# A feed-forward that starts on a quarter of its modulation, and attention with v as the stationary operand

## The chip, the core and the metric

The kernel runs on one core of a Trainium2 chip. The metric is the device time in microseconds (us) from the first to the last instruction of one launch. Each engine (TensorE for matmuls, VectorE, ScalarE, GpSimd, and SyncE, which issues DMAs) works through its own queue in the order in which the program gives it instructions; semaphores make one wait for another.

## The reference

One step of a small diffusion backbone of two layers: 256 latent and 128 context tokens of width 1024 (three tiles of 128 tokens, NT = 3). Per layer: a SwiGLU feed-forward, a mixer (layer 0 attention, layer 1 a gated recurrence) and a second feed-forward, each between two RMS norms and with a modulation made from a conditioning vector. What the change touches is the first feed-forward and the attention:

```python
mod = (silu(c) @ w_ada[i] + b_ada[i])                  # shift, scale, gate for three sub-layers
h = rmsnorm(x, g_pre) * (1 + scale) + shift            # D_MODEL = 1024
a, b = split(h @ w_in);  out = (silu(a) * b) @ w_out   # D_FF = 2816
# attention: 16 query heads of 64, 4 key/value heads, one softmax with a sink per head
s = concat([q @ k_window.T, q @ k_ctx.T]) * 64 ** -0.5
m = maximum(max(s), sink);  e = exp(s - m)
o = (e @ v) / (sum(e) + exp(sink - m))
```

Latent queries see 256 latent keys (masked to a window) and 128 cached context keys, so 384 keys; context queries see 128.

## The kernel before

**Weights.** All big weights are streamed through one list, `chunks`, of 512 KB pieces, each a 128x1024 tile. SyncE loads a chunk into a raw buffer (L172); `w_split` makes two parts of it, `wh` on ScalarE (L198, a rounded copy) and `wl` on VectorE (L199, the rest; on GpSimd where `ws["eng"]` says so), and a product in nearly full precision is three matmuls of the rounded parts (`mm3`, L451 to L453). `take` gives the next chunk and splits it if that has not been done; `prefetch` splits some chunks ahead. Chunks in `plain` are used as they are. The first NE chunks go through ten buffers (`early`: one raw, three slots, three `araw`, `gbr`, two raws), the later ones through three raws; a buffer is loaded anew when its last reader is done.

**The start.** `start` loads x and the conditioning, normalises x and turns it (`normalise`, `lay`), and computes shift and scale of the first feed-forward in two halves of 512 features: `gather` (sixteen plain chunks of `w_ada`, two matmuls each into 32-partition rows of a PSUM bank), an evacuation on ScalarE (L1430), `spread` (four tiny matmuls that turn the rows into columns), then `modulate_first` (scale and shift on VectorE L1458, rounded copy on ScalarE L1463, rest on VectorE L1467). Two feed-forward chunks that need only the first half run before the second half's modulation (`between`), a third is used as filler (`fill`).

**The feed-forward.** 44 chunks of `w_ffn_in`, each 24 matmuls of 128x384, in 11 groups of four; after each group a gate (silu and product). Then 22 chunks of `w_ffn_out`. Between the chunks `pace` puts pieces of the other modulations: a unit (`ada_unit`) multiplies a 128x1024 tile of `w_ada` by a column and adds it up on VectorE (L247); sixteen units are one kind, and a kind ends with a rows matmul (L272), an evacuation and small DMAs. `set_pace` gives the number of kinds that should be ready: 5 in the first feed-forward, 5.5 and 6 in attention.

**Attention.** After the projections (`qkv_part`, `q_evac`, `kd_turn`) the queries are turned (`q_turn`). The loop runs over 36 items: 16 single heads of tile 0, four items of four heads of the context tile, 16 heads of tile 1. For an item: `score` (two matmuls and a mask, TensorE), `top` and `shift` (maximum, VectorE), `expo` (ScalarE, with the sum), `flip` (transposes of e, TensorE, and the evacuation to `pT` on ScalarE, L954), `weigh` (pT is the stationary operand, v moves, 64 columns each). Scores run two items ahead, exponentials one. After eight heads `o_prep`, `o_norm` (division, L977), `o_turn` (transposes), `o_hi`, `o_lo` bring the output into `hT`.

## Time and profile before

| | |
|---|---|
| median of three runs | 1585.67 us (1583.9 to 1587.08) |
| the profiled execution | 1587.23 us, its span 1585.5 us |
| mean granted TensorE clock | 0.995 |
| TensorE busy | 1549.3 us, 98% of the span |
| VectorE busy | 1046.4 us, 66% |
| ScalarE busy | 651.6 us, 41% |

The span is the time from the first to the last instruction of the profiled execution. An engine's busy time is the time in which at least one of its instructions was running.

### The profile page before, as it was taken

How to read it: one execution, taken by the hardware profiler on the slowest of the kernel's cores; microseconds unless marked ns; L12 is line 12 of the kernel's file. 1: busy time of each engine (PE TensorE's matmuls, PEld its weight loads, DVE VectorE, ACT ScalarE, POOL GpSimd, SP SyncE). 2: the span in 40 equal slices, each digit the busy share in tenths (PEclk: the TensorE clock that was granted, in tenths of full speed). 3: DMA queues.
4: the chain of work that ended last, by engine and by line, in shares of the span. 5: the costliest groups of instructions: out<-in, count | busy, mean ns of one | idle time of the engine just before them, and what ended most of it. 6: DMA issues, size and time to landing. Idle time of an engine off the chain costs nothing.

```text
span 1585.5 us, 22547 instructions
## 1 busy us (share of the span) xinstructions
PE 1549.3 (98%) x8798; PEld 1414.8 (89%) x8798; DVE 1046.4 (66%) x1388; ACT 651.6 (41%) x1118; POOL 161.7 (10%) x308
## 2 busy tenths in 40 slices
PE   6999999998999999999999999999999999999997
PEld 4899998887879999988999998899999889999985
DVE  3787788577756777785688889666666764333452
ACT  3423233365745322334523233356655443323441
POOL 1111111000011111120111111110000110000000
PEclk9999999999999999999999999999999999999999
DMA  8777667342224766665377776634333335433321
GB/s 307 245 242 219 221 214 239 120 146 81 67 94 138 218 216 206 207 215 180 114 235 228 227 236 229 227 106 134 101 113 100 121 113 163 130 126 127 131 96 40
DMA packets 164091, 264.50 MB, mean 167 GB/s; under 512 B 10432, under 2 KB 122144, under 8 KB 163984
## 3 DMA queue, kind: packets, MB, share of 16 engines
q1 hardware_dynamic: 140592, 187.27, 36.4%
q0 software_dynamic: 22864, 75.36, 14.8%
q8 instruction: 69, 1.13, 0.3%
q10 hardware_dynamic: 528, 0.43, 0.1%
q14 instruction: 38, 0.31, 0.1%
HBM read 260.01 MB, written 3.01 MB: 166 GB/s over the span
## 4 chain that ended last, share of the span: by engine, by line
PE 92%; DVE 4%; ACT 2%; issue 1%; DMA 0%; POOL 0%; DVEq 0%; POOLq 0%; ACTq 0%
PE pb L451 14%; PE pb L452 14%; PE pb L453 14%; PE pb L461 14%; PE pb L463 13%; PE pb L466 13%; PE pb L963 1%; PE pb L272 1%; PE pb L953 1%; PE pb L923 1%; PE pb L1132 1%; DVE slot L247 1%; PE pb L434 1%; DVE wl L199 1%; PE pb L1428 1%
## 5 line engine op out<-in xcount | busy, mean ns | idle before, releaser
L198 ACT ACTIVATE wh<-raw 128x1024 fp32r<-128x1024 f32 x247 | 259.8, 1058 | 413.2 <-PE pb L466 254.8
L461 PE MATMUL pb<-hT,wh 128*128 128x384 f32 (+1 forms) x1248 | 410.2, 332 | 0.0
L199 DVE TENSOR_TENSOR wl<-raw,wh 128x1024 fp32r<-128x1024 f32 x245 | 298.5, 1223 | 167.7 <-ACT wh L198 167.2
L463 PE MATMUL pb<-hT,wl 128*128 128x384 f32 (+1 forms) x1248 | 406.5, 329 | 0.0
L247 DVE SCALAR_TENSOR_TENSOR slot<-araw,sc,slot 128x1024 f32<-128x1024 f32 x224 | 281.5, 1279 | 0.0
L466 PE MATMUL pb<-hT,wh 128*128 128x384 f32 (+1 forms) x1248 | 259.8, 329 | 0.0
L461 PEld LDWEIGHTS pb<-hT,wh 128*128 128x128 f32 x1248 | 234.8, 188 | 6.2 <-issue 5.9
L463 PEld LDWEIGHTS pb<-hT,wl 128*128 128x128 f32 x1248 | 234.9, 188 | 0.2
L466 PEld LDWEIGHTS pb<-hT,wh 128*128 128x128 f32 x1248 | 215.8, 188 | 0.0
L451 PE MATMUL pb<-wh,gh 128*128 128x512 f32 x384 | 150.6, 392 | 0.2 <-DVE dump L282 0.2
L452 PE MATMUL pb<-wl,gh 128*128 128x512 f32 x384 | 149.6, 389 | 0.0
L453 PE MATMUL pb<-wh,gl 128*128 128x512 f32 x384 | 149.5, 389 | 0.0
L233 POOL DMA_DIRECT2D araw<-in_w_ada_dram x128 | 68.7, 537 | 578.0 <-DVE slot L247 480.6
L451 PE MATMUL pb<-hT,wh 128*128 128x384 f32 x352 | 119.7, 340 | 4.9 <-ACT hT L1463 4.9
L452 PE MATMUL pb<-hT,wh 128*128 128x384 f32 x352 | 119.0, 338 | 0.2 <-DVE hT L1467 0.2
L453 PE MATMUL pb<-hT,wl 128*128 128x384 f32 x352 | 118.6, 337 | 0.0
L199 DVE TENSOR_TENSOR wl<-araw,wh 128x1024 fp32r<-128x1024 f32 x52 | 63.6, 1224 | 68.3 <-ACT wh L198 68.3
L451 PE MATMUL pb<-wh,hT 128*128 128x512 f32 (+1 forms) x258 | 94.3, 365 | 1.1 <-ACT sgn L1242 0.9
L453 PE MATMUL pb<-wh,hT 128*128 128x512 f32 (+1 forms) x258 | 90.7, 352 | 0.0
L452 PE MATMUL pb<-wl,hT 128*128 128x512 f32 (+1 forms) x258 | 90.6, 351 | 0.0
L451 PEld LDWEIGHTS pb<-wh,gh 128*128 128x128 f32 x384 | 72.1, 188 | 19.4 <-issue 3.4
L453 PEld LDWEIGHTS pb<-wh,gl 128*128 128x128 f32 x384 | 72.1, 188 | 15.2
(242 smaller groups left out, 2177.8 us busy)
## 6 DMA issues: line engine op xcount, KB each, us to landing
raw<-in_w_ffn_in_dram SPq DMA_DIRECT2D x155, 512.0 KB, 4.4
araw<-in_w_ada_dram POOLq DMA_DIRECT2D x128, 512.0 KB, 4.4
raw<-in_w_ffn_out_dram SPq DMA_DIRECT2D x76, 512.0 KB, 4.2
raw<-in_w_rec_in_dram SPq DMA_DIRECT2D x21, 512.0 KB, 3.6
araw<-in_w_ffn_in_dram SPq DMA_DIRECT2D x21, 512.0 KB, 3.5
araw<-in_w_rec_in_dram SPq DMA_DIRECT2D x19, 512.0 KB, 3.7
slot<-dsc POOLq DMA_DIRECT2D x24, 256.0 KB, 5.2
raw<-in_w_qkv_dram SPq DMA_DIRECT2D x12, 512.0 KB, 4.1
```

The source lines that it names most:

```text
L198: S.activation(out=h, in_=r, func=AF.Copy)
L199: ws["eng"].tensor_tensor(out=lo, in0=r, in1=h.bitcast(F32), op=ALU.subtract)
L233: G.dma_start(out=araw[j % NA], in_=w_ada[kd[0], (j % 8) * P:(j % 8 + 1) * P, acol(kd):acol(kd) + 1024])
L247: V.scalar_tensor_tensor(out=acc[v], in0=src, scalar=s_, in1=acc[v], op0=ALU.mult, op1=ALU.add)
L272: T.matmul(out=bank[32 * r:32 * r + 32, :], lhsT=ones, rhs=acc[v][:, 512 * h:512 * h + 512], start=True, stop=True, skip_group_check=True,)
L434: T.transpose(bks[half][:, k * P:(k + 1) * P], src[:, kk * P:(kk + 1) * P], ident)
L451: T.matmul(out=out, lhsT=a[0], rhs=b[0], start=start, stop=False, skip_group_check=True)
L452: T.matmul(out=out, lhsT=a[0], rhs=b[1], start=False, stop=False, skip_group_check=True)
L453: T.matmul(out=out, lhsT=a[1], rhs=b[0], start=False, stop=stop, skip_group_check=True)
L461: T.matmul(out=out, lhsT=a[0], rhs=b[0], start=start, stop=False, skip_group_check=True)
L463: T.matmul(out=out, lhsT=x, rhs=y, start=False, stop=False, skip_group_check=True)
L466: T.matmul(out=out, lhsT=x, rhs=y, start=False, stop=stop, skip_group_check=True)
```

## The change

In the start, shift and scale are made in four quarters of 256 features instead of two halves: a plain chunk now holds four k-blocks of 256 columns, a `gather` is four matmuls of 256 columns, and one bank (PB[7]) holds both kinds. `between` is written out by hand: it takes the eight chunks of the first two groups (f00 to f03 and f10 to f13, the first digit the group) and runs `unit`s, six matmuls over the two k-blocks of one quarter. x is loaded on SyncE's queue ahead of the chunks, no longer on GpSimd's. NE is 22. The first feed-forward makes six kinds of modulation, attention none.

In attention `weigh` runs once per eight heads, with v (128x64) as stationary operand and 512 columns of `pT` moving; the result is already turned, so 1/den is spread over 64 columns, transposed (`o_row`) and multiplied in (`o_mul`) before `o_hi` and `o_lo`. Scores run three items ahead, exponentials two; two of five evacuations of `flip` go to VectorE; the first three scores are put between the last three `qkv_part`s of the context tile, and six of the query transposes into the loop (`q_turn4`). The rows of `w_attn_out` come in another order, in two DMAs per chunk.

```diff
-NE = 18
-PLAIN = tuple(range(8)) + tuple(range(10, 18))
+NE = 22
+PLAIN = tuple(6 * q + i for q in range(4) for i in range(4))
...
+    for q in range(4):
         for kind in (1, 0):
+            col = kind * 1024 + 256 * q
+            early_chunks += [av[0][:, 4 * h:4 * h + 4, col:col + 256] for h in range(2)]
+        early_chunks += chunks[4 * (q % 2) + 2 * (q // 2):][:2]
...
+            if isinstance(c_, tuple):
+                for q in range(2):
+                    SP.dma_start(out=raw_of(j)[64 * q:64 * q + 64, :], in_=c_[q])
...
+            def unit(gi, s, m, w, kq):
...
+                for k in (2 * kq, 2 * kq + 1):
+                    group.append((bank(gi, m, s)[:, 0:TOK], (wv[0][:, k % 4, ms], wv[1][:, k % 4, ms]), (hT[:, :, 0, k, :], hT[:, :, 1, k, :]),
+                                  k == 0, k == KD - 1))
+                mm3s(group, "a")
...
-        set_pace(5.5, 9)
+        set_pace(6, 5)
...
-            def weigh(i):
...
-                            out=bank(6 + h // 8)[:, (h % 8) * 64:(h % 8) * 64 + 64], lhsT=src[:, o:o + P],
-                            rhs=v_sb[:, k0 + j, (h // 4) * 64:(h // 4) * 64 + 64], start=j == 0, stop=j == n - 1,
+            def weigh(t, gp, c):
+                n, k0 = (3, 0) if t < 2 else (1, 3)
+                for j in range(n):
+                    for q in range(2):
                         T.matmul(
+                            out=bank(6 + c % 2)[64 * q:64 * q + 64, :], lhsT=v_sb[:, k0 + j, (2 * gp + q) * 64:(2 * gp + q) * 64 + 64],
+                            rhs=pT[c % 2][:, 4 * q:4 * q + 4, j, :], start=j == 0, stop=j == n - 1, skip_group_check=True,
...
+                if i % 5 in (1, 3):
+                    V.tensor_copy(out=dst, in_=src)
+                else:
+                    S.activation(out=dst, in_=src, func=AF.Copy)
...
+            def o_mul(t, gp, c):
+                u = half_of(slots[oslot], c % 2)
+                S.activation(out=u, in_=bank(5), func=AF.Copy)
+                V.tensor_tensor(out=u, in0=u, in1=bank(6 + c % 2), op=ALU.mult)
...
+                    for lag, step, fn in ((0, 1, o_prep), (1, 0, weigh), (1, 1, o_den), (3, 0, o_row), (3, 1, o_mul), (4, 0, o_hi), (4, 1, o_lo)):
...
+            for i in range(3):
                 score(i)
                 top(i)
                 shift(i)
+                if i > 0:
+                    expo(i - 1)
+                qkv_part(2, 1 + i, ww[i], sets[2][2])
...
             for i in range(n + 1):
+                if i + 2 < n:
+                    expo(i + 2)
                 if i < n:
                     flip(i)
+                if i + 3 < n:
+                    score(i + 3)
                 fire(i, 0)
+                if i + 3 < n:
+                    top(i + 3)
+                    shift(i + 3)
                 fire(i, 1)
...
+        def between(unit, gate):
+            ws["eng"] = G
+            (f00,) = take()
+            ws["eng"] = V
+            modulate_first(0)
+            (f01,) = take()
+            laid(1)
+            for s, w in ((0, f00), (1, f01)):
+                for m in range(2):
+                    unit(0, s, m, w, 0)
+            for i in range(4):
+                gather(1, i, 0)
+            (f10,) = take()
+            unit(1, 0, 0, f10, 0)
+            spread(1)
+            unit(1, 0, 1, f10, 0)
             modulate_first(1)
+            (f11,) = take()
+            unit(1, 1, 0, f11, 0)
+            for m in range(2):
+                unit(0, 0, m, f00, 1)
+            for i in range(4):
+                gather(2, i, 0)
+            for m in range(2):
+                unit(0, 1, m, f01, 1)
+            spread(2)
+            for s, m, w in ((0, 0, f10), (0, 1, f10), (1, 0, f11)):
+                unit(1, s, m, w, 1)
+            (f02,) = take()
+            modulate_first(2)
+            (f03,) = take()
+            for s, w in ((0, f02), (1, f03)):
+                for m in range(2):
+                    unit(0, s, m, w, 2)
+            for i in range(4):
+                gather(3, i, 0)
+            (f12,) = take()
+            for m in range(2):
+                unit(1, 0, m, f12, 2)
+            spread(3)
+            modulate_first(3)
+            for kq in range(2):
+                unit(1, 1, 1, f11, kq)
+            (f13,) = take()
+            w_split(24, 12)
+            for s, w in ((0, f02), (1, f03)):
+                for m in range(2):
+                    unit(0, s, m, w, 3)
+            gate(0, TOK)
+            w_split(26, 18)
+            for m in range(2):
+                unit(1, 1, m, f13, 2)
+            for s, w in ((0, f12), (1, f13)):
+                for m in range(2):
+                    unit(1, s, m, w, 3)
+            gate(1, TOK)
...
-        done = ffn(0, 0, 5, None, [0, 1, 2, 3], between)
+        done = ffn(0, 0, 6, None, [0, 1, 2, 3], between)
```

## Rows read from the trace of the kernel before

**Rows 1.** The page, part 4: the chain of work that ended last, shares of the span by engine.
```profile
PE 92%; DVE 4%; ACT 2%; issue 1%; DMA 0%; POOL 0%; DVEq 0%; POOLq 0%; ACTq 0%
```

**Rows 2.** Stretches of the start: from and to (us), length, busy time (and instructions) of each engine, granted TensorE clock, DMA share, GB/s.
```profile
0.00:10.00 10.00, 2.13 (x5) 0.27 (x5) 1.84 (x4) 3.82 (x10) 3.73 (x14) 1.00 0.76 267
...
20.00:30.00 10.00, 6.14 (x34) 4.06 (x35) 5.86 (x16) 3.85 (x11) 2.34 (x1) 0.81 1.06 382
```

**Rows 3.** Timeline of the start: start (us), duration, engine, line, operation, tiles, count, in brackets the idle time of the engine just before and what ended it.
```profile
7.64 1.88 PE L1428 MATMUL pb<-raw,sc 128*2 128x512 f32 x4 [0.27 <-DVE sc L1419]
...
19.06 0.60 ACT L1430 ACTIVATE slot<-pb 128x512 f32<-128x512 f32 x1 [6.42 <-PE pb L1428]
...
22.62 0.60 ACT L1430 ACTIVATE slot<-pb 128x512 f32<-128x512 f32 x1 [2.48 <-PE pb L1428]
...
24.24 2.34 POOL L199 TENSOR_TENSOR wl<-raw,wh 128x1024 fp32r<-128x1024 f32 x1 [10.57 <-ACT wh L198]
...
26.83 1.13 ACT L1463 ACTIVATE hT<-slot 128x256 fp32r<-128x256 f32 x4 [2.66 <-DVE slot L1458]
...
27.49 0.69 PE L451 MATMUL pb<-hT,wh 128*128 128x384 f32 x1 [3.17 <-ACT hT L1463]
...
33.26 0.34 PE L453 MATMUL pb<-hT,wl 128*128 128x384 f32 x1
...
38.46 0.34 PE L453 MATMUL pb<-hT,wl 128*128 128x384 f32 x1
...
38.73 0.60 PE L1428 MATMUL pb<-raw,sc 128*2 128x512 f32 x2
...
41.42 1.05 PE L1437 MATMUL pb<-cf,slot 128*128 128x2 f32 x8
...
50.43 0.45 PE L451 MATMUL pb<-hT,wh 128*128 128x384 f32 x1 [1.71 <-ACT hT L1463]
...
53.78 0.34 PE L451 MATMUL pb<-hT,wh 128*128 128x384 f32 x1
```

**Rows 4.** Timeline, one split of a chunk and one pair of modulated blocks (columns as in rows 3).
```profile
30.10 1.04 ACT L198 ACTIVATE wh<-raw 128x1024 fp32r<-128x1024 f32 x1
...
31.17 1.23 DVE L199 TENSOR_TENSOR wl<-raw,wh 128x1024 fp32r<-128x1024 f32 x1 [0.30 <-ACT wh L198]
...
50.95 0.66 DVE L1458 TENSOR_SCALAR slot<-slot,slot 128x256 f32<-128x256 f32 x2
...
51.39 0.62 ACT L1463 ACTIVATE hT<-slot 128x256 fp32r<-128x256 f32 x2 [0.50 <-DVE slot L1458]
```

**Rows 5.** The page, part 6: DMA issues by tile, count, KB each, median us from issue to landing.
```profile
raw<-in_w_ffn_in_dram SPq DMA_DIRECT2D x155, 512.0 KB, 4.4
...
raw<-in_w_rec_in_dram SPq DMA_DIRECT2D x21, 512.0 KB, 3.6
```

**Rows 6.** One head of the steady loop in the chain of waits (start, us on the chain, what), and the groups of the loop's stretch, 383.5 to 447.5 us, on ScalarE and VectorE (busy us, mean ns of one, idle time before them and what ended it).
```profile
391.55 0.33 PE pb L953 x3
391.88 0.34 PE pb L923 x2
392.30 0.67 PE pb L963 x6
...
L943 ACT ACTIVATE p<-pb,nm 128x384 f32<-128x384 f32 x32 | 18.6, 580 | 11.3 <-DVE nm L935 10.6 <-DVE den L975 0.6
L930 DVE TENSOR_REDUCE mx<-pb 128x1 f32<-128x384 f32 x32 | 17.8, 555 | 12.1 <-PE pb L926 11.8
L954 ACT ACTIVATE pT<-pb 128x384 f32<-128x384 f32 x32 | 15.6, 487 | 0.3 <-PE pb L953 0.3
```

**Rows 7.** Timeline of ScalarE in the loop: an evacuation, an exponential, an evacuation, each right behind the other.
```profile
423.27 0.48 ACT L954 ACTIVATE pT<-pb 128x384 f32<-128x384 f32 x1
...
423.64 0.58 ACT L943 ACTIVATE p<-pb,nm 128x384 f32<-128x384 f32 x1
...
424.19 0.50 ACT L954 ACTIVATE pT<-pb 128x384 f32<-128x384 f32 x1
```

**Rows 8.** Timeline of TensorE around the loop: the last query transposes ahead of the context tile's query parts, the flips of items 8, 16, 20 and 28, and the first product of the output projection.
```profile
372.05 1.94 PE L885 MATMUL pb<-cf,qs 128*128 128x128 f32 x16
...
397.25 0.50 PE L953 MATMUL pb<-cf,p 128*128 128x128 f32 x3
...
410.12 1.34 PE L953 MATMUL pb<-cf,p 128*128 128x128 f32 x4
...
420.14 0.55 PE L953 MATMUL pb<-cf,p 128*128 128x128 f32 x3
...
434.54 0.49 PE L953 MATMUL pb<-cf,p 128*128 128x128 f32 x3
...
447.54 0.48 PE L451 MATMUL pb<-wh,hT 128*128 128x512 f32 x1
```

**Rows 9.** Timeline of TensorE at a rows matmul: four matmuls of 512 columns (two records each) on four groups of 32 columns, and the operation behind them.
```profile
449.11 1.06 PE L272 MATMUL pb<-slot,ones 128*32 128x512 f32 x8
450.11 0.50 PE L451 MATMUL pb<-wh,hT 128*128 128x512 f32 x1
```

**Rows 10.** Stretches of the first feed-forward at the turn to its output half (columns as in rows 2; the third busy time is VectorE's).
```profile
210.00:230.00 20.00, 19.84 (x113) 18.00 (x112) 19.03 (x25) 8.86 (x15) 3.74 (x7) 1.00 0.62 204
230.00:250.00 20.00, 20.00 (x90) 16.54 (x89) 17.57 (x19) 7.39 (x10) 2.74 (x5) 1.00 0.71 239
```

More of the change, by code (lines that the diff above doesn't have):

```diff
@@ L620, in products @@
                     groups.append(group)
-                if side:
-                    mm3s([g_ for pair in zip(*groups) for g_ in pair], None)
-                    return
                 for group in groups:
@@ L663, in ffn @@
             n = 0
[L664 removed]
             while n < len(order):
[L666 removed]
+                gi, kp = order[n]
                 if n == len(order) - 2:
@@ L705, in ffn @@
                 prefetch()
-                products(gi, kp, w, 0, NT, side=n == 3 and between is not None)
+                products(gi, kp, w, 0, NT)
                 if n == 4 and between is None:
@@ L1398, in start @@
         G.memset(mhalf, -0.5)
-        for kind in range(2):
-            V.memset(PB[6 + kind], 0.0)
+        V.memset(PB[7], 0.0)
         S.activation(out=stat[:, 0, :], in_=ones[:, 0:8], func=AF.Silu)
```

283 lines of the change are left out of this document (116 added, 167 removed).

## Prediction

> **What bounds the kernel now.** I read the page's chain of waits first: TensorE holds 92% of what ended last [rows 1]. A change pays only where TensorE stands still, runs at its lower clock, or does fewer matmuls. Next I read the timeline of the two stretches that the diff touches.
>
> In the start the reader is to see that the first product of the feed-forward (a 128x384 matmul, L451) runs at 27.49 us, the fourth chunk's first at 50.43, and that from 53.78 the products follow one another without a gap [rows 3]. Two chunks of 24 and two halves of 12 (72 products) precede 50.43, and 15 more 53.78. At 0.173 us each (the 18th starts at 33.26, the 48th at 38.46), eight chunks (192 products, what the new opening holds) are through at 53.78 + 105 x 0.173 = 72.0 us. That is the mark for the opening.
>
> In attention the marks are the sixteen transposes that end at 373.7 and the first product of the output projection at 447.54, 73.8 us later [rows 8]. In the steady part the chain is TensorE's alone: per head transposes 0.33, scores 0.34 (0.42 with the mask), weighing 0.67, together 1.43 [rows 6]. The weighing is the dearest.
>
> **The change: the opening.** Bytes and sums stay: 16 chunks of modulation weights, 16 x 2 x 512 columns of gathers, four spreads. What changes is their order.
>
> *First product.* The three x blocks (1.57 MB) now go ahead of chunk 0 on SP's queue. In the first 10 us 2.67 MB arrived [rows 2], so 2.1 MB are there at about 8.5, usable near 9.5 (estimate), against a first gather at 7.6 before. Four gathers and three layings then take TensorE about 8.2 us, less than the 11.4 of before (7.6 to 19.06) because nothing waits for x and four column groups run at a time. The evacuation of the first quarter falls at 18.0 to 18.3 instead of 22.62 for both kinds. From that evacuation the way is as before: wh on ScalarE 1.05, wl on GpSimd 2.34 during which VectorE's L1458 stands (first pair free only at 26.83), then the product: 27.49 - 22.62 = 4.87 [rows 3]. So 23.0 us, 4.5 earlier; I allow 22.3 to 24.
>
> *From there I walk along TensorE's order.* Prices: product 0.173; gather 0.45 a chunk (six chunks from 38.73 to 41.42); spread 1.0; evacuation 0.6; wh 1.05 and wl 1.23 with some 0.1 of hand-over; per pair of modulated blocks 0.66 on VectorE, 0.62 on ScalarE [rows 3, 4]. No chunk is split ahead any more: each take() stands right before its use, behind the evacuation or the modulation in ScalarE's order.
> - 24 products of quarter 0. The first 17 were slow after 27.49 (until 33.26, 5.8 us; the granted clock was 0.81 on the mean of that stretch, a mix of 1.2 and 2.4 GHz [rows 2, 3]); the idle ahead is like that of before, so again: 23.0 + 5.8 + 7 x 0.173 = 30.0.
> - Four gathers 1.8: 31.8. Then f10's wh stands behind the evacuation: **wait 1.8**; four products, **wait 0.6** for wl, two products, spread, six products: 37.2.
> - f11's wh stands behind all of modulate_first(1): from the spread's end 0.1 + 0.6 (three small operations) + 0.66 + 0.62 + 0.62 + 1.05 + 0.1 = 3.75, of which six products cover 1.04: **wait 2.7**, then **0.6** for wl: 41.6.
> - 12 products, gathers, 12, spread, 18 products: 51.6. Quarter 2's blocks come 0.1 + 0.6 + 1.23 (f02's wl ahead of them on VectorE) + 0.66 + 0.62 after the spread, nearly hidden under the 18: **wait 1.1** in all; 24 products: 56.9.
> - Gathers 1.8: 58.7. f12 is chunk 22, and its buffer (raws[1]) is that of chunk 19, which the second of these gathers reads. So its DMA starts at 57.8, lands 3.6 later (the quickest median; 4.4 is the commonest [rows 5]), and needs 1.05 of ScalarE: **wait 3.9**, then **0.6**; 12 products, spread, 12 products of f11: 68.4.
> - **Wait 1.3** for quarter 3's blocks, 24 and 36 products: 80.1.
>
> So 80.1 against 72.0: **8.1 us later**. The sum of its parts: first product -4.5; waits behind it 12.6 against 2.7 before (1.9 ahead of 50.43 and 0.8 behind it); three spreads and twelve gathers instead of two and eight, +2.8; that is 8.2. If the 3.9 us wait is followed by the slow clock as the 3.2 us one ahead of 27.49 was (the 1.9 us one ahead of 50.43 was not), 2.4 more. I take 8.5, with 4 (landing at 3, two waits half hidden) and 12 (slow clock, the ada DMAs of GpSimd in the way of f12) as ends.
>
> **The change: pacing.** Attention loses 16 units of modulation (1.28 us each on VectorE); the first feed-forward has 96 instead of 80 on 36 instead of 41 chunk steps. VectorE is busy 19.0 of 20 us at the turn to the output half and 17.6 after it [rows 10], and gets 10% more work: about full. Cover: weights are split up to four chunks (16 us) ahead, so I price it at nothing; uncovered it costs up to 3 us. The rows matmul of the sixth kind (1.0 us, [rows 9]) moves with it, no gain. The output weights now come in two DMAs a chunk: eight issues more on SP, whose queue is nearly idle there; nothing to 0.5 us.
>
> **The change: attention.** *Weighing.* Before, 6 records of 64 columns a head, 0.67. After, for eight heads 6 matmuls of 512 columns with v stationary, in pairs on two halves of the array's columns. No row shows halves; the nearest are four matmuls of 512 columns on four column groups, 1.0 us from the first to the next operation [rows 9]. Side by side a pair costs 0.9: 2.7 for eight heads instead of 5.4, and 12.6 instead of 25 for the whole loop. One after the other 1.8 each: no gain. I take 0.9. *Added:* per eight heads two small VectorE copies (0.3 each), one more ScalarE copy (0.5); 2 of 5 evacuations go from ScalarE to VectorE. *Moved:* three scores and six of the query transposes go into and under the loop, with three query parts (1.38 each) between the scores.
>
> TensorE's work from 373.7 on thus falls to 51 us: transposes 12.5, scores 16.7, query parts 4.1, query transposes 2.6, weighing 12.6, transposes of 1/den 2.6. But it has to be fed in order: exp(i+2), copy(i) on ScalarE; top, shift, some copies on VectorE. Per group of eight heads ScalarE needs 8 x 0.56 + 5 x 0.38 + 1.2 = 7.6 us, VectorE 8 x 0.60 + 3 x 0.47 + 2.4 = 8.6 (0.56 and 0.38 from start to start [rows 7]; VectorE's 0.60 is its reduction and what follows it [rows 6]), TensorE 9.2; every one of them is near the bound. And the weighing is now one block of 2.7 us that stands between flip(i) and flip(i+1): ScalarE has two exponentials and a copy ready (1.5 us), then waits 1.5 for the flip and 0.8 for the next shift; the normalisation goes ScalarE, VectorE, ScalarE, VectorE, each in its queue's order, some 2 us more of waits. I wrote the loop down queue by queue with these durations, each operation starting when its queue and its inputs are free. The loop of before comes out so at 64.6 us, where the trace has 64.0. The new one, from 373.7:
> - until flip 8: 15.9 (before: 397.25 - 373.7 = 23.5): **-7.6**, the fill of the pipe and the query transposes;
> - flip 8 to 16: 14.0 (12.9); 16 to 20: 8.9 (10.0); 20 to 28: 15.5 (14.4); 28 to the end: 15.2 (13.0) [rows 8]: **+3.3**, as the block's waits eat what the cheaper weighing gives.
>
> So 69.5 against 73.8: **-4.3 us**. Ends: -18 (no engine waits, below) and +6 (pairs in series: the same walk with 1.8 gives 79.8).
>
> This is where a rule speaks against the change. The Trainium skill, TensorEngine Tiling (Array Packing), Performance Considerations (PSUM Bottleneck), says that tiling quickens TensorE but not the evacuation of PSUM, which may become the bottleneck. By that rule alone the loop could not end before VectorE's 45 us (36 maxima, 14 evacuations, two splits, six times 2.4) and its waits are through, which is what my walk has; no run here shows it yet.
>
> **Sum.** The profiled execution took 1587.23 us, 1.56 above the median shown. 1587.2 + 8.5 - 4.3 = 1591.4; against the median 1589.9, so **1590 us**. Measurement tells about 0.2%, 3.2 us.
>
> **Rivals.**
> - *The loop runs at TensorE's pace* (the other side). If three scores and two exponentials ahead are enough to bridge the 2.7 us block, the loop needs 51 + some 4 of filling and ending: 18 to 19 us less; with the opening at +8.5, 1576. For: each engine's sum is below 9.3 a group. Against: ScalarE and VectorE are in order and trade four times per group. It decides from a loop of 62 us on (373.7 to about 436). Chance 0.17.
> - *The opening is even* (its waits are covered, say because f12 lands in time): -4.3 alone, 1581.5. Against: the order of take() on ScalarE. Chance 0.12.
> - *The two cancel*: opening +5, attention -5, 1586. Chance 0.18.
> - *Pairs in series*: +8.5 + 6, 1600. For: no row with halves; against: the four groups ran together. Chance 0.10.
> - *My forecast*, 1587 to 1596: 0.43.
>
> The range 1576 to 1600 leaves out half of the first and of the fourth. My own case alone has its 1587 to 1596. Faster by over 0.2%: the first, the second less a third, 0.25. Within: the third and a slice of mine, 0.25. Slower: the rest, 0.50.
>
> **What would show it.** Opening right: first product near 23, then waits of 1.8, 2.7 and 4 us from about 32, 37 and 59 on, the last ending on a DMA of w_ffn_in; 192 products through near 80 to 82. Attention right: the weighing's pairs 0.9 apart, an eight-head group of 13 to 15 us, TensorE's transposes waiting for ScalarE's and VectorE's copies. Wrong: f12's weights there before the fourth gather, or TensorE without gaps in the loop; then the time falls below 1582.

## The result and the profile after

The changed kernel takes 1605.2 us (median of four runs, 1604.8 to 1606.3), the kernel before 1586.4 (four runs): ratio 1.0125, 95% interval 1.0113 to 1.0138. It is 19 us slower, and the forecast of 1590 us (1576 to 1600) missed it on the fast side. The profiled execution took 1605.46 us, its span 1603.7, the mean granted clock 0.985 (before 0.995). The chain of waits, by engine (compare [rows 1]: TensorE held 92%, DMAs 0%):

```profile
PE 90%; DVE 3%; ACT 2%; issue 2%; DMA 2%; POOL 0%; SPq 0%; DVEq 0%; POOLq 0%; ACTq 0%
```

**Where the time went.** I cut both traces at six marks of TensorE (start times) and compare the stages.

| stage | ends at (before, after) | length before | after | difference |
|---|---|---|---|---|
| to the first product | 27.49, 22.31 | 27.49 | 22.31 | -5.2 |
| to the record with the 192nd product | 71.80, 85.44 | 44.31 | 63.13 | +18.8 |
| rest of the input half | 227.31, 241.25 | 155.51 | 155.81 | +0.3 |
| output half of the first feed-forward | 321.17, 346.11 | 93.86 | 104.86 | +11.0 |
| attention, to the output projection | 447.54, 468.60 | 126.37 | 122.49 | -3.9 |
| output projection, to the third eight turns of the next norm | 494.33, 513.90 | 46.79 | 45.30 | -1.5 |

A row of the trace can hold two products: in the new order the 191st and the 192nd stand in one row, whose start counts, 0.17 us early. Behind the last mark the distance stays (1234.52 and 1254.07 at a wait in the recurrence) but for 1.4 us at the very end. These 1.4 are not the change's: from that wait to the end the profiles of all kernels here show either 349.3 to 349.7 or 350.7 to 351.0 us, with the old parts and with the new. So the opening costs 13.6 us and the output half 11.0, and attention with its projection gives 5.4 back.

*The opening.* Timeline of the changed kernel's start (columns as in [rows 3]; L464 to L469 are the products there, L201 the rounded copy of a split, L1440 the spread, L175 and L236 the loads of SP and GpSimd), then stretches of it (columns as in [rows 2]).

```profile
22.31 0.69 PE L464 MATMUL pb<-hT,wh 128*128 128x384 f32 x1 [3.59 <-ACT hT L1469]
...
32.61 0.44 PE L464 MATMUL pb<-hT,wh 128*128 128x384 f32 x1 [1.66 <-ACT wh L201]
33.87 1.01 PE L469 MATMUL pb<-hT,wl 128*128 128x384 f32 x2 [0.30 <-DVE wl L202]
34.67 1.70 PE L1440 MATMUL pb<-cf,slot 128*128 128x2 f32 x8
...
39.52 0.69 PE L464 MATMUL pb<-hT,wh 128*128 128x384 f32 x1 [1.02 <-ACT wh L201]
...
56.33 1.83 POOL L236 DMA_DIRECT2D araw<-in_w_ada_dram  x3
58.80 1.49 SPq L175 DMA_DIRECT2D raw<-in_w_ffn_in_dram  x3
64.53 1.06 ACT L201 ACTIVATE wh<-raw 128x1024 fp32r<-128x1024 f32 x1 [4.20 <-DMA raw<-in_w_ffn_in_dram]
65.64 0.69 PE L464 MATMUL pb<-hT,wh 128*128 128x384 f32 x1 [6.03 <-ACT wh L201]
71.86 0.69 PE L464 MATMUL pb<-hT,wh 128*128 128x384 f32 x1 [0.52 <-DVE slot L1450]
...
85.44 0.51 PE L469 MATMUL pb<-hT,wl 128*128 128x384 f32 x2
```

```profile
30.00:40.00 10.00, 7.02 (x41) 5.46 (x32) 4.45 (x13) 3.68 (x7) 0.00 (x0) 0.69 0.97 312
40.00:50.00 10.00, 10.00 (x71) 8.54 (x71) 0.72 (x1) 1.55 (x2) 0.00 (x0) 0.80 0.18 56
...
60.00:70.00 10.00, 4.36 (x15) 4.24 (x15) 1.22 (x1) 1.39 (x2) 0.00 (x0) 0.73 0.86 302
70.00:80.00 10.00, 9.48 (x46) 9.39 (x46) 5.90 (x15) 5.69 (x10) 0.00 (x0) 0.76 0.26 76
```

The reader sees each wait of the walk: 1.66 for f10, 1.02 for f11, 6.03 for f12, whose load starts at 58.80, behind three loads of GpSimd at 56.33, and is there at 64.5. And the reader sees what the walk had nearly left out: behind the waits for f10 and for f12 the clock falls (at the one for f11 it is down already). Between 30 and 80 us the granted clock is 0.69 to 0.80 in four of five stretches (a mix of 1.2 and 2.4 GHz), and a spread takes 1.70 us instead of 1.05 [rows 3].

*The output half.* The two waits of the changed kernel (timeline; L454 is the product, L275 the rows matmul of a kind).

```profile
244.78 0.50 PE L454 MATMUL pb<-wh,gh 128*128 128x512 f32 x1 [1.98 <-DVE dump L285]
310.80 3.08 PE L275 MATMUL pb<-slot,ones 128*32 128x512 f32 x8 [3.96 <-DVE slot L250]
```

One stretch of it, in the changed kernel and then in the kernel before (columns as in [rows 2]).

```profile
250.00:300.00 50.00, 50.00 (x224) 40.17 (x223) 44.16 (x48) 19.54 (x26) 9.59 (x18) 1.00 0.75 258
```

```profile
250.00:300.00 50.00, 50.00 (x224) 40.17 (x223) 30.93 (x35) 18.34 (x26) 6.72 (x13) 1.00 0.59 193
```

VectorE's costliest group from the first output product to the first product of attention, after and before (columns as in [rows 6]).

```profile
L250 DVE SCALAR_TENSOR_TENSOR slot<-araw,sc,slot 128x1024 f32<-128x1024 f32 x27 | 33.6, 1278 | 0.0
```

```profile
L247 DVE SCALAR_TENSOR_TENSOR slot<-araw,sc,slot 128x1024 f32<-128x1024 f32 x14 | 17.5, 1278 | 0.0
```

The output half has 27 of these units instead of 14; VectorE is busy 44.2 of 50 us instead of 30.9. TensorE never waits for split weights there. It waits for a modulation that nobody needs yet: at the rows matmul, which stands in its queue, until VectorE has done the last unit (4.0 us), and for a bank that VectorE has still to read (2.0). The 1.06 us matmul of [rows 9] then takes 3.08: the granted clock is 0.53 there, and its second pair starts 1.2 us after the first, since it needs one unit more. Of the 11.0 us, 5.8 are standing still (5.9 against 0.2), 1.1 is the rows matmul that moved here, and the rest, some 4, is mostly the lower clock around the two waits (0.81 on the mean from 241 to 250 us, 0.96 from 300 to 346; an estimate).

*Attention.* The marks of [rows 8] in the changed kernel, in order of time: sixteen transposes, flips 8 and 16, the second weighing of eight latent heads (L956, six matmuls in twelve records), flips 20 and 28, the third weighing, the last one, the first product of the output projection.

```profile
396.99 1.91 PE L877 MATMUL pb<-cf,qs 128*128 128x128 f32 x16
...
414.86 0.50 PE L944 MATMUL pb<-cf,p 128*128 128x128 f32 x3
...
428.71 0.66 PE L944 MATMUL pb<-cf,p 128*128 128x128 f32 x4 [1.02 <-ACT qs L950]
...
430.14 3.64 PE L956 MATMUL pb<-qs,v_sb 128*64 128x512 f32 x12
...
437.95 0.50 PE L944 MATMUL pb<-cf,p 128*128 128x128 f32 x3
...
452.26 0.50 PE L944 MATMUL pb<-cf,p 128*128 128x128 f32 x3
...
453.11 2.98 PE L956 MATMUL pb<-qs,v_sb 128*64 128x512 f32 x12
...
463.84 4.82 PE L956 MATMUL pb<-qs,v_sb 128*64 128x512 f32 x12
468.60 0.50 PE L454 MATMUL pb<-wh,hT 128*128 128x512 f32 x1
```

From the transposes' end (396.99 + 1.65, as 372.05 + 1.65 before): 16.2 to flip 8, then 13.9, 9.2, 14.3 and 16.3, together 70.0; the walk had 15.9, 14.0, 8.9, 15.5, 15.2, together 69.5. The four weighings take 2.9, 3.6, 2.9 and 4.8 us to the next operation, where 2.7 was the price; the second runs at full clock (1.00), the last at a granted clock of 0.64, behind three waits of the loop's end. TensorE waits 8.7 us in this stretch, 6.5 of them for the evacuations of flip on ScalarE (L950) and VectorE (L948); from 373.7 to 447.54 in the kernel before it waits 5.9 us, none of it for the evacuation of flip (L954). Its waits from 398.6 to 468.6 us (us in total, times, longest):

```profile
PE pb L944 <- ACT qs L950: 4.7, 6, 1.2
PE pb L944 <- DVE qs L948: 1.8, 3, 0.8
```

### The profile page after: what moved, and what is told of

Read it like the earlier page. It is cut to its first block, busy times and chain, and to the rows that moved or that the text cites. A ratio compares the mean times of both kernels' runs of the same rounds, so it can differ in the third digit from the quotient of the medians.

```text
span 1603.7 us, 22376 instructions
## 1 busy us (share of the span) xinstructions
PE 1549.7 (97%) x8694; PEld 1405.4 (88%) x8694; DVE 1053.6 (66%) x1420; ACT 648.9 (40%) x1110; POOL 158.3 (10%) x304
## 4 chain that ended last, share of the span: by engine, by line
PE 90%; DVE 3%; ACT 2%; issue 2%; DMA 2%; POOL 0%; SPq 0%; DVEq 0%; POOLq 0%; ACTq 0%
PE pb L464 14%; PE pb L466 14%; PE pb L469 14%; PE pb L454 13%; PE pb L456 13%; PE pb L455 13%; PE pb L275 1%; PE pb L956 1%; DVE slot L250 1%; DMA raw<-in_w_ffn_out_dram 1%; PE pb L1134 1%; PE pb L406 0%; PE pb L1426 0%; DVE wl L202 0%; ACT wh L201 0%
## 5 line engine op out<-in xcount | busy, mean ns | idle before, releaser
L464 PE MATMUL pb<-hT,wh 128*128 128x384 f32 (+1 forms) x1312 | 436.4, 336 | 12.8 <-ACT wh L201 8.7
L201 ACT ACTIVATE wh<-raw 128x1024 fp32r<-128x1024 f32 x242 | 254.6, 1058 | 411.6 <-PE pb L469 255.6
L202 DVE TENSOR_TENSOR wl<-raw,wh 128x1024 fp32r<-128x1024 f32 x242 | 294.5, 1223 | 157.9 <-ACT wh L201 155.2
L464 PEld LDWEIGHTS pb<-hT,wh 128*128 128x128 f32 x1312 | 249.6, 190 | 21.2 <-ACT wh L201 10.2
L469 PE MATMUL pb<-hT,wh 128*128 128x384 f32 (+1 forms) x1248 | 259.8, 329 | 0.0
L469 PEld LDWEIGHTS pb<-hT,wh 128*128 128x128 f32 x1248 | 215.8, 188 | 0.0
L454 PE MATMUL pb<-wh,gh 128*128 128x512 f32 x384 | 151.3, 394 | 2.0 <-DVE dump L285 2.0
L236 POOL DMA_DIRECT2D araw<-in_w_ada_dram x128 | 68.7, 537 | 510.5 <-DVE slot L250 416.5
L454 PE MATMUL pb<-hT,wh 128*128 128x384 f32 x288 | 96.9, 336 | 0.0
L456 PE MATMUL pb<-hT,wl 128*128 128x384 f32 x288 | 96.3, 334 | 0.0
L455 PE MATMUL pb<-hT,wh 128*128 128x384 f32 x288 | 96.3, 334 | 0.0
L454 PE MATMUL pb<-wh,hT 128*128 128x512 f32 (+1 forms) x258 | 93.8, 363 | 1.1 <-ACT sgn L1244 0.9
L454 PEld LDWEIGHTS pb<-wh,gh 128*128 128x128 f32 x384 | 72.4, 189 | 20.5 <-issue 3.4
L456 PEld LDWEIGHTS pb<-wh,gl 128*128 128x128 f32 x384 | 72.5, 189 | 15.3
```

Source lines behind the costliest of these rows:

```text
L201: S.activation(out=h, in_=r, func=AF.Copy)
L202: ws["eng"].tensor_tensor(out=lo, in0=r, in1=h.bitcast(F32), op=ALU.subtract)
L236: G.dma_start(out=araw[j % NA], in_=w_ada[kd[0], (j % 8) * P:(j % 8 + 1) * P, acol(kd):acol(kd) + 1024])
L454: T.matmul(out=out, lhsT=a[0], rhs=b[0], start=start, stop=False, skip_group_check=True)
L455: T.matmul(out=out, lhsT=a[0], rhs=b[1], start=False, stop=False, skip_group_check=True)
L456: T.matmul(out=out, lhsT=a[1], rhs=b[0], start=False, stop=stop, skip_group_check=True)
```

## The experiments

Stage lengths of all runs (us; opening from the first product to the 192nd, output half, attention, output projection as above), median, and ratio to the kernel before on the same chip with its 95% interval. Its own median lay at 1584.5 to 1585.1 there. The start of the first product differs by up to 2.4 us between runs of one opening (22.3 to 24.7), so single profiles are compared by lengths. These scatter too: the changed opening takes 62.3 to 66.2 us where it stands as it is, the new attention without units 121.1 to 123.6. Three kernels compute something else than the reference: pieces divides some groups of heads by other groups' sums, splits_ahead and mended multiply by weights of later chunks.

| kernel | first product | opening | output half | attention | projection | median | ratio |
|---|---|---|---|---|---|---|---|
| before | 27.5 | 44.3 | 93.9 | 126.4 | 46.8 | | |
| after | 22.3 | 63.1 | 104.9 | 122.5 | 45.3 | 1605.2 | 1.0125 (1.0113-1.0138) |
| pacing_alone | 26.7 | 43.9 | 97.5 | 123.8 | 45.1 | 1584.6 | 0.9995 (0.9986-1.0003) |
| pacing_back | 23.8 | 64.8 | 101.1 | 129.9 | 46.8 | 1612.3 | 1.0168 (1.0154-1.0181) |
| old_opening | 28.1 | 44.4 | 97.5 | 122.5 | 45.2 | 1584.9 | 1.0001 (0.9992-1.0009) |
| attention_alone | 27.3 | 44.2 | 93.9 | 130.1 | 46.8 | 1589.4 | 1.0023 (1.0013-1.0033) |
| f12_buffer | 24.2 | 56.0 | 104.9 | 121.1 | 45.4 | 1600.2 | 1.0092 (1.0078-1.0105) |
| rate_44 | 24.7 | 66.2 | 101.6 | 123.4 | 45.3 | 1606.0 | 1.0131 (1.0115-1.0146) |
| pieces | 27.9 | 44.4 | 97.5 | 121.5 | 45.4 | 1584.8 | 0.9999 (0.9991-1.0008) |
| one_half | 27.1 | 44.0 | 97.5 | 122.9 | 45.1 | 1586.4 | 1.0002 (0.9993-1.0011) |
| splits_ahead | 23.2 | 57.5 | 103.3 | 121.1 | 45.2 | 1600.8 | 1.0102 (1.0088-1.0115) |
| rows_late | 22.5 | 62.3 | 107.4 | 121.7 | 45.2 | 1613.7 | 1.0183 (1.0169-1.0197) |
| pieces_b | 27.4 | 44.4 | 97.5 | 122.4 | 45.2 | 1585.0 | 0.9997 (0.9988-1.0006) |
| mended | 22.8 | 57.6 | 108.9 | 121.4 | 45.3 | 1606.9 | 1.0137 (1.0122-1.0153) |
| opening_ahead | 22.9 | 45.6 | 105.0 | 123.6 | 45.3 | 1591.2 | 1.0035 (1.0021-1.0049) |
| all_mended | 22.6 | 45.5 | 100.6 | 124.1 | 46.8 | 1589.6 | 1.0025 (1.0015-1.0036) |
| units_in_projections | 26.4 | 43.6 | 94.1 | 122.8 | 46.8 | 1581.9 | 0.9984 (0.9975-0.9992) |
| old_loop | 26.1 | 43.7 | 94.1 | 123.5 | 46.7 | 1582.4 | 0.9988 (0.9978-0.9998) |
| both | 22.7 | 45.4 | 95.1 | 123.3 | 46.8 | 1581.9 | 0.9982 (0.9973-0.9991) |


### Taking the change apart

**pacing_alone** is the kernel before with six kinds in the first feed-forward and none in attention.

```diff
-        done = ffn(0, 0, 5, None, [0, 1, 2, 3], between)
+        done = ffn(0, 0, 6, None, [0, 1, 2, 3], between)
-        set_pace(5.5, 9)
+        set_pace(6, 5)
-            set_pace(6, 30)
```

> The kernel before with the pacing of the change alone: six kinds of modulation in the first feed-forward, none in attention. Theory A (VectorE is overfull in the output half whatever the opening): the two waits of TensorE for VectorE there (2.0 and 4.0 us in the changed kernel) and the slow clock behind them come back, some +9 us, less 1.5 for the rows matmul that leaves the output projection: 1592 to 1596 us. Theory B (the overload comes from the opening, which takes five paced steps away and pushes ten units, 12 us of VectorE, from the input half into the output half): with the old opening 41 steps carry 79 of the 96 units and the rest is done by the ninth output chunk, so 1585 to 1589 us.

Theory B was right in the sum: no difference (1584.6, just below its range). But it is a sum: +3.6 in the output half, where this is the wait left (timeline),

```profile
233.61 2.25 PE L272 MATMUL pb<-slot,ones 128*32 128x512 f32 x8 [1.27 <-DVE slot L247]
```

and -2.6 in attention, which is still the old loop, and -1.7 in the output projection, where a kind's rows matmul no longer falls. So the old loop seems to pay for its units (old_loop below shows 2.9, each in one profile), and I had put that at nothing.

**pacing_back**: the changed kernel with the pacing of before (five kinds; `set_pace(5.5, 5)`, `set_pace(6, 30)` and `pace()` in the loop).

> The changed kernel with the pacing of before: five kinds in the first feed-forward, eight units in the projections and eight in the loop of attention. If the pacing costs what the marks of the output half say (+11 there, of which 1.1 is the rows matmul that is only moved): 1605 - 10 = 1595 us, plus what the loop pays for eight units of 1.2 us on VectorE. Theory C (VectorE is near its bound in the new loop): the loop is 5 to 8 us longer, 1600 to 1603 us. Rival (the units fit beside the loop): 1595 to 1597 us.

Neither: 1612.3. The output half is 3.8 shorter, not 10, since with eight unpaced chunks even 80 units leave too much for it. And attention is 7.4 us longer, the upper end of theory C.

**old_opening**: the changed kernel with `start`, `between` and the chunk list of before.

> The changed kernel with the opening of before (two halves, first product at 27.5 us); pacing and attention as changed. If the three parts simply add: 1605.2 - 13.8 = 1591.4 us. Theory B (the opening is also what overfills the output half): the waits for VectorE at the turn and at the sixth rows matmul go too, 1581 to 1585 us.

1584.9: with the opening all of the loss goes, 20.3 us, of which 12.9 are in the opening itself (72.5 instead of 85.4 us to the 192nd product) and 7.4 in the output half (97.5 instead of 104.9). Theory B: the opening's own order takes five paced steps away and pushes their units into the output half. What remains, the new attention and its pacing, is worth nothing together.

**attention_alone**: attention's part of the diff on the kernel before, units as in pacing_back.

> The kernel before with the attention part of the change alone: eight units in the projections, eight in the loop. If the units are hidden there: 1586.4 - 4 (the marks of the two traces) = 1582 us. Theory C (the new loop has no room on VectorE, its gain was bought with the units that left): the loop is 5 to 8 us longer than in the changed kernel, 1587 to 1590 us, no gain.

1589.4, +0.23%, in the range of theory C. With units in the loop the new attention is 3.7 us slower than the old one. VectorE's groups in the loop (columns as in [rows 6]; L253 is the unit, L934 the maximum, L961 the evacuations it has taken over):

```profile
L934 DVE TENSOR_REDUCE mx<-pb 128x1 f32<-128x384 f32 (+1 forms) x36 | 20.3, 565 | 6.9 <-PE pb L930 6.7
L253 DVE SCALAR_TENSOR_TENSOR slot<-araw,sc,slot 128x1024 f32<-128x1024 f32 x8 | 10.2, 1277 | 0.0
L961 DVE COPY qs<-pb 128x384 f32<-128x384 f32 (+1 forms) x14 | 8.0, 571 | 0.6 <-ACT qs L963 0.3 <-PE pb L957 0.2
```

And one of the waits that result (timeline):

```profile
422.67 0.55 PE L957 MATMUL pb<-cf,p 128*128 128x128 f32 x3 [2.22 <-ACT qs L963]
```

Eight units, 10.2 us on VectorE, cost this loop 7.3 us (130.1 against 122.8 in units_in_projections), the old loop 2.9 (126.4 against 123.5 in old_loop).

**one_half**: old_opening with the weighing's two loops exchanged, so that three matmuls stand on one half of the array before three on the other.

```diff
-                for j in range(n):
-                    for q in range(2):
+                for q in range(2):
+                    for j in range(n):
```

> The changed kernel with the opening of before (1584.9 us), and the weighing's six matmuls ordered half by half: three on one half of the array's columns, then three on the other, the same matmuls. If the pairs of the change run side by side because neighbours stand on different halves: a block takes 3 x 1.9 = 5.4 instead of 2.9 us, the loop is some 10 to 13 us longer, 1595 to 1598 us. Rival (a matmul of 512 columns costs the same in any order): the blocks stay at 2.9 us, 1584 to 1586 us.

```profile
393.73 3.71 PE L969 MATMUL pb<-qs,v_sb 128*64 128x512 f32 x12
```

Neither: each of the four blocks takes 3.6 us to the next operation, and the time does not change. The records of a block say why. They form two chains of six, 0.43 us from start to start in each, as much beside the other chain as ahead of it; that a chain is one half of the array is read from this spacing, since the trace does not name the half. In the change's order the second chain starts 0.2 us after the first: a matmul, two records, holds its half for 0.86 us, both halves work side by side, and three pairs with their end take 2.9. In half order the second chain starts 0.91 us after the first, which has three records still to start, so the halves overlap here too. The edit therefore did not put the pairs in series, and my expectation that it would was wrong; six matmuls one behind the other would take about 5.2 us (6 x 0.86, an estimate). The pairs do run side by side. Nor does the order alone set the length of a block: in the changed kernel's second block (430.14 above) the second chain starts 0.85 late as well, and the last block, 4.8 there, is 3.6 here at a clock of 1.00. The four blocks together take 14.6 us here and 14.2 in old_opening.

**pieces** and **pieces_b**: old_opening with the block cut in three.

```diff
+                    cut = t < 2 and i < n - 1
+                    for j in range(3 if cut else 1):
+                        events.setdefault((i + 1 + j, 0), []).append((weigh, args + ([j] if cut else [0, 1, 2],)))
```

> The changed kernel with the opening of before (1584.9 us), and the weighing of a latent group of eight heads in three pieces of one pair (0.97 us), one behind each of three flips, instead of a block of 2.9; the last group stays a block. Theory F (the block starves ScalarE and VectorE, each waiting for the next flip and score): the queue walk gives 64.4 instead of 69.5 us from the last query transposes on, so -5, 1580 us. Rival (the normalisation, which goes back and forth between four queues, sets the pace): 0 to -1, 1584 to 1585 us.

> As pieces (the opening of before, the weighing of a latent group in three pieces of one pair), with the steps of the normalisation where the changed kernel has them. The first form, which also put the transposes of 1/den one item later, behind the next group's 1/den, and so normalised some groups with the wrong ones, gave 0 to -0.3 us. Walk: 66.9 instead of 70.3 us from the last query transposes on, -3.4, 1581.5 us. Rival (the handshakes of the normalisation set the pace): 1584 to 1585 us.

Theory F fell: 122.4 instead of 122.5, no gain in the time. The walk was right to 0.5 us for the block and off for the pieces by 3.0 us (pieces_b, 69.9 for 66.9) and 4.6 (pieces, 69.0 for 64.4). What sets the pace of the second half is not settled by these two; the cut shows only that the block alone does not.

### The opening

**f12_buffer**: one number, so that f12 and f13 find buffers that are free earlier.

```diff
-NE = 22
+NE = 24
```

> The changed kernel (1605.2 us) with NE = 24 instead of 22: f12 and f13 go into buffers that the third quarter's gathers leave free, so f12's load can start some 7 us earlier. Theory D (the late load of f12 costs the opening its 6.0 us wait and, through the lower clock behind it, 4.4 us more): no wait at f12, 192 products through near 75.5 instead of 85.8, the time 1594 to 1596 us. Theory E (the three loads of modulation weights on GpSimd's queue at 56.3 us share the DMA engines with f12, wherever its buffer is): the wait shrinks only by 2 to 3 us, the clock still falls, 1600 to 1602 us.

```profile
63.64 0.44 PE L464 MATMUL pb<-hT,wh 128*128 128x384 f32 x1 [1.72 <-ACT wh L201]
...
80.12 0.51 PE L469 MATMUL pb<-hT,wl 128*128 128x384 f32 x2
```

```profile
63.64:80.60 16.96, 16.14 (x93) 15.73 (x94) 10.22 (x19) 7.61 (x13) 0.00 (x0) 1.00 0.61 199
```

The 6.0 us wait becomes 1.7, now for ScalarE and not for the load, and the clock no longer falls behind it (second fence): 7.2 us off the opening, 5 of them in the time (the first product came 1.9 later in this profile). The time lies in the range of theory E, but what E says does not happen; D is right about the load and left out the wait for the split. And a wait of 1.72 us with one of 0.29 behind it, as long as those for f10 (1.66 and 0.30), leaves the clock at 1.00 here, so its length alone does not bring the clock down.

**splits_ahead** was to remove the other waits by splitting f10, f11, f02 and f12 ahead of the gathers; there the loads overran chunks that the gathers had not read, so that these read other weights and waited for them.

> The changed kernel with NE = 24 (1600.2 us by itself), and f10 and f11 split ahead of the second quarter's gathers, f02 ahead of the third's, f12 ahead of the fourth's, so that none of these splits stands behind an evacuation on ScalarE. Theory D (what is left of the opening's loss is the waits for splits, 1.7 + 0.3, 1.0 and 1.7 + 0.3 us, and the low clock from 36 to 44 and up to 50 us behind them): from the first product to the 192nd 46 to 48 instead of 56 us, the time 1590 to 1592 us. Theory E (the low clock there follows the gathers and spreads themselves, not the waits): only the 5 us of waits go, 1595 us.

It says nothing for either theory. **opening_ahead** holds the loads back (the cut shows the second quarter; the third and the fourth are alike, with f02 and f12, and NE is 24):

```diff
+            ws["cap"] = 16
+            w_split(11, 6)
             for i in range(4):
                 gather(1, i, 0)
+            ws["cap"] = 10 ** 9
+            w_ahead()
```

> As splits_ahead (the changed kernel with NE = 24, and f10, f11, f02 and f12 split ahead of the gathers), but with the loads held back to the buffers whose chunk the gathers have read; in splits_ahead the loads overran four unread chunks, whose gathers then read other weights and waited 4.8 and 3.3 us for them. f12_buffer alone has 56.0 us from the first product to the 192nd, the opening of before 44.4. Theory D (waits for splits behind evacuations and the low clock behind them): 46 to 49 us, the time 1591 to 1593 us. Theory E (the low clock follows the gathers and spreads themselves): 51 to 53 us, 1595 to 1597 us.

Its timeline, and two of its stretches (columns as above):

```profile
22.94 0.69 PE L464 MATMUL pb<-hT,wh 128*128 128x384 f32 x1 [3.59 <-ACT hT L1469]
56.30 0.44 PE L464 MATMUL pb<-hT,wh 128*128 128x384 f32 x1 [0.60 <-DVE slot L1450]
68.55 0.51 PE L469 MATMUL pb<-hT,wl 128*128 128x384 f32 x2
```

```profile
30.00:40.00 10.00, 9.95 (x102) 7.32 (x94) 3.94 (x12) 2.75 (x6) 0.00 (x0) 1.00 1.00 317
40.00:50.00 10.00, 10.00 (x67) 9.73 (x60) 5.09 (x13) 3.64 (x7) 2.04 (x3) 1.00 0.51 163
```

Theory D, in full: with the same gathers, spreads and products the opening takes 45.6 instead of 63.1 us, its only wait above 0.5 us is one of 0.60, and the clock stays at 1.00 from 30 us on. The 192nd product is 3.3 us ahead of the kernel before. So the waits for splits and loads were the cause of the low clock, and both together of the opening's loss; which of the short waits it takes, f12_buffer leaves open. The output half keeps its 105.0 us, which makes this kernel 0.35% slower still.

### The output half

**rate_44** deals the units out over 44 steps instead of 50 (`set_pace(n_kinds, 44)`), **rows_late** puts the rows matmul four steps behind its last unit (`max(ad["wait"], 4)`, for every kind of the kernel); each on the changed kernel.

> The changed kernel with the units of modulation dealt out over 44 steps instead of 50 (2.2 instead of 1.9 a chunk), so that the input half of the first feed-forward does 79 of the 96 units, as it does with the old opening. Theory B (the new opening pushes ten units into the output half, and that costs 7.4 us of its 11.0): output half 97 to 98 us instead of 104.9, the time 1598 us. Rival (VectorE is then overfull in the input half, and TensorE waits there for the split weights): what is won in the output half is lost ahead of it, 1603 to 1607 us.

> The changed kernel (1605.2 us) with the rows matmul of each kind put four steps behind its last unit instead of one. Theory G (VectorE is not overfull over the output half, where it has 70 us of work in 105, but it runs behind its program order, and TensorE, in order too, stands at the rows matmul until the last unit is through): the wait of 4 to 4.7 us and the doubled 3.1 us matmul behind it go, output half 97 to 99 instead of 104.9 us, the time 1598 us. Theory B as it stood (VectorE is overfull there, so the lag only moves to the next handshake): output half 103 to 105 us, 1604 to 1606 us.

```profile
256.60 2.96 PE L275 MATMUL pb<-slot,ones 128*32 128x512 f32 x8 [4.29 <-DVE slot L250]
```

```profile
332.32 0.28 PE L301 MATMUL pb<-cf,r 32*128 32x32 f32 x1 [3.69 <-DMA r<-dsc]
```

At the higher rate (first fence) the input half is as long as ever (155.8), so the rival's reason is wrong, but the lag meets another kind's rows matmul: 3.3 us gained there, a wait for f12 of 7.1 instead of 6.0 in this profile, and nothing of it in the time (1606.0, in the rival's range). With the later matmul (second fence) TensorE waits less at it (2.8) and then for the small DMAs that follow it, and the stretch from the first eight turns of the next norm to the wait in the recurrence, which is 762.8 to 763.0 us in the kernels without this edit, is 6.2 longer. Theory G fell: a lag only moves the wait to the next handshake.

**mended** was splits_ahead, rows_late and pieces_b in one.

> The changed kernel with all three: splits ahead and NE = 24, rows matmuls four steps later, the weighing in pieces. If the losses are the ones named and add up: 1605.2 - 14 (opening) - 7 (output half) - 2 (attention) = 1582 us, level with or just below the kernel before. If the losses only move to the next wait: 1590 to 1596 us.

It has splits_ahead's overrunning loads too, and the losses only moved: output half 108.9, and the time above both ranges.

**units_in_projections** is old_opening with five and a half kinds in the first feed-forward and eight units in the projections of attention, **old_loop** the kernel before with the same (and the other two lines of pacing_alone), **all_mended** and **both** are opening_ahead with the same at 40 and 44 steps.

```diff
-        done = ffn(0, 0, 6, None, [0, 1, 2, 3], between)
+        done = ffn(0, 0, 5.5, None, [0, 1, 2, 3], between)
```

> The changed kernel with the opening of before (1584.9 us), five and a half kinds in the first feed-forward and eight units in the projections of attention, none in the loop. If the loop's loss in attention_alone (130.1 us from the first projection product to the output projection, against 122.5 without units) comes from the eight units in the loop alone: 123 to 125 us here, output half 95 to 96 instead of 97.5, the time 1584 us. If those in the projections cost as much: 126 to 127 us, 1587 us.

> opening_ahead, with five and a half kinds in the first feed-forward, dealt out over 40 steps, and the last eight units in the projections of attention, none in the loop. If VectorE's lag at the turn and in the output half is what the units left over there make: output half 95 to 98 instead of 104.9 us, projections 51 to 53, loop as in the changed kernel (71.6): 1584 to 1588 us. If the lag is made by the rate: output half 100 to 103, 1590 to 1594 us.

> The kernel before with the units placed as in units_in_projections (five and a half kinds in the first feed-forward, eight units in the projections, none in the loop) and nothing else changed. If the gain of units_in_projections (1581.9 against 1584.5 us) is the new attention's: 1584 us here, as before. If it is the units' absence from the loop: the old loop too gains the 2.6 us that pacing_alone showed (123.8 instead of 126.4 us from the first projection product to the output projection), and the time is 1582 to 1583 us.

> opening_ahead (192nd product 3.3 us ahead of the kernel before) with the units as in units_in_projections, dealt out over 44 steps, so that the input half ends at the same unit (72 of 88) as there. all_mended, at 40 steps, ended it at the 79th, and the fifth kind's rows matmul then stood at the turn, where VectorE also prepares the first eight pairs of the output half, and waited 3.2 us. If the place of that matmul made the 100.6 us of its output half: 94 to 95 us, the time 1578 to 1580 us. If the opening with eight unpaced chunks costs the output half in any case: 98 to 101 us, 1584 to 1588 us.

The projections take the eight units for nothing (122.8), and with 88 units the output half is 94.1, as before. old_loop gains as much as units_in_projections within what can be told: 123.5 against 122.8, so the new attention by itself is worth 0.6 us here and 1.3 in the first batch (122.5 against 123.8), both less than one attention differs by between profiles, and the medians too show no gain (0.9984 against 0.9988, 1.0001 against 0.9995). all_mended and both differ in the steps alone. At 40 steps a rows matmul stands at the turn and waits 3.2 us, and the output half takes 100.6 us, though fewer units are left for it than before (12 instead of 14, counted as above). In both, at 44 steps, with 16 units left, it takes 95.1, and the matmul waits 0.6. So the number of units left over does not decide by itself; place and rate moved together here, and which of them does is not shown. The rows of both:

```profile
68.13 0.51 PE L469 MATMUL pb<-hT,wl 128*128 128x384 f32 x2
...
243.81 2.25 PE L275 MATMUL pb<-slot,ones 128*32 128x512 f32 x8 [0.62 <-DVE slot L250]
```

both, old_loop and units_in_projections are all below the kernel before, by 0.12 to 0.18%, less than the 0.2% that the prediction took as what can be told; their intervals lie below 1, but overlap one another. The shortest edit among them, three lines of pacing in old_loop, has most of it. The time of both, 1581.9, is 2 us above the range expected for it.

## Why the prediction was wrong, point by point

The direction was right; the sum (+8.5 - 4.3) was to be +13.6 + 0.3 + 11.0 - 3.9 - 1.5, and 1.4 at the end went off by chance.

- **First product at 23.0**: 22.31. Right.
- **Waits of the opening, 12.6**: 9.5 (1.66, 0.30, 1.02, 6.03, 0.52). Right in place and cause; the wait for f11 was smaller (2.7 forecast), f12's larger (3.9), since its load started 1.0 later and took 5.7 us to land behind GpSimd's three, not 3.6, which I had named for the upper end only.
- **The slow clock, 2.4 at most and 0.4 in the sum**: here the step failed. From 13.6 = -5.2 + 6.8 (waits, 9.5 against 2.7) + 2.8 (spreads and gathers) + rest, the rest is 9.2 us. The clock was at half (0.50) from 34.67 to 43.84 and from 65.64 to 74.60, 18.1 us in which TensorE worked 16.6; half of that, 8.3, is the estimate of what it cost. I had given the low clock to f12's wait alone, with 0.4 us of it in the sum, because a 1.9 us wait of before had not brought it. Behind the waits of 1.66 and 0.30 for f10 it came all the same. opening_ahead shows that without the waits it does not come; why 1.72 and 0.29 in f12_buffer do not bring it stays open.
- **Pacing priced at nothing, up to 3**: the step that failed most. "Weights are split up to four chunks ahead" covers the split weights, and it did. It does not cover TensorE's own instructions that wait for VectorE, the rows matmul, which has one step of lead, and the product that needs the bank which VectorE reads last. I read VectorE's 17 to 19 of 20 us [rows 10] as "about full" and did not ask who else waits for it. Nor did I count that the units which the opening no longer takes land in the output half: 27 instead of 14 (the number alone does not decide, as all_mended shows). The two edits, priced singly, had no joint row: 3.6 us with the old opening, 11.0 with the new.
- **"No gain" for the moved rows matmul**: 1.5 to 1.7 us less in the output projection, and as much or more in the output half, where the matmul now stands (3.08, and a wait of 3.96). No gain in the sum was right, no loss was not.
- **Attention -4.3**: -3.9, with the stations right to 1.2 us each. But the reason was wrong for the greater part, and the number partly luck. I gave all of it to the change of the loop; 2.6 go with the units that left it (pacing_alone), and the 1.3 left for the loop are within the scatter of profiles. The weighing's price, 2.7 a block, held for two blocks of four. That I held the old loop's units for hidden, with VectorE at 37 of 50 us there, is the same error as above.
- **The rule that evacuation may become the bound** (the Trainium skill, TensorEngine Tiling (Array Packing), Performance Considerations (PSUM Bottleneck)): the traces agree. TensorE's share became cheaper, 6.5 of its 8.7 us of waits in the loop now end on evacuations, and 10.2 us of other VectorE work cost 7.3 us instead of 2.9.
- **The rivals**: the loop at TensorE's pace did not come (70.0, not 62); pairs in series fell with the 2.9 us block, and the records in one_half show the halves side by side; the two did not cancel; the even opening came only in opening_ahead. None of them held the output half, and so the range ended 5 us short.

## What to carry to other kernels

Where an engine is near 90% busy, the buffer ahead of its main consumer does not cover the others: list every instruction of the bounding engine that waits for it, and give each its own lead or move the work to a stage with room. When a new order takes steps away from a background task, ask where its units go next, and price the two edits together. Waits in this opening cost more than twice, once themselves (6.8 us more than before) and once by the clock behind them (some 8), so split and load ahead of them before the order is judged.

## What was not expected of the hardware

- The waits of 1.66 and 0.30 us for f10 were followed by 9.2 us at a granted clock of 0.50, the 6.03 us wait for f12 by 9.0 us at 0.50; the same work without them ran at 1.00 (opening_ahead). Waits of 1.72 and 0.29 in f12_buffer, and of 1.71 and 0.21 in the kernel before ([rows 3], at 50.43), were not followed by a lower clock. The Trainium skill says (TensorE: Matmul & The Clock Gate, HAM oscillation) that a long wait for data brings the clock down and that the next burst then starts slow. The trace agrees for the 6.03 us wait; its example has no waits as short as those for f10.
- Two matmuls of 512 columns on the two halves of the array's columns take 0.97 us together in turn (a third of 2.9, end included), and one holds its half for 0.86 us (two records, 0.43 apart): side by side is worth a factor of 1.8 here, also in half order, where the second half's matmuls began 0.91 us after the first half's.
- A 512 KB load issued behind three others landed after 5.7 us, where its median is 4.5 on the page of the same profile.
